# Query head norm moved from the queries to the exponential: a per-token scale instead of a per-column factor, in the attention stage of a decoder step

## The chip, the core and the metric

The kernel runs on one core of one Trainium2 chip. The core has a matrix engine (PE, TensorE), a vector engine (DVE), a scalar engine (ACT), GpSimd (POOL), a sync engine (SP) that issues nearly all DMAs here, 16 DMA engines, an on-chip memory with 128 partitions (SBUF) and matrix-product buffers (PSUM). Each engine runs its own instructions in its own order and waits on semaphores for the others. The metric is the device time of one execution in microseconds (us); lower is better.

## The reference, cut to what matters

One step of a two-layer decoder trunk over 512 prompt tokens and 32 sample tokens (8 requests of 4), model width 1024, 8 heads of 128. The first layer ends with a shared key, value and log-forget value; the second layer attends to them. The change is in the attention of the second layer:

```python
q = rmsnorm((xn @ att_w_q[j]).reshape(bsz, L, N_HEADS, HEAD_DIM), q_norm[j])
...
s = jnp.einsum('bqhd,bkhd->bhqk', qb, k).astype(jnp.float32) * scale      # scale = HEAD_DIM ** -0.5
s = s + cq[..., :, None] - csum[..., None, :]                             # csum: running sum of log-forget
s = jnp.where(causal[None, None], s, -jnp.inf)
p = jax.nn.softmax(s, axis=-1).astype(v.dtype)
return jnp.einsum('bhqk,bkhd->bqhd', p, v)
```

`rmsnorm` divides each query, per token and head, by the root of the mean square of its 128 values and multiplies by a gain per value. The sample tokens do the same against 256 cached keys and 4 own ones.

## The kernel before, in words

Everything is held transposed: 128 features on the partitions, the 544 tokens (512 + 32) along the free axis. Every large product is done in three matmuls: each operand is split into a rounded high part (fp32r) and the remainder, and high x high, high x low and low x high are summed in PSUM (lines L285, L289, L291 for a projection tile: 8 blocks of the inner dimension x 3 x 2 column halves of 272 = 48 matmuls). ACT makes the high part, DVE subtracts for the low part (L241 and L242 for weights, L329 and L330 for activations, L341 and L342 where a gain goes in).

Buffers come from pools: 45 of a large kind (`big`), 8 of a token-row kind (`tmp`), 3 two-bank PSUM tiles (`ps`) and 2 one-bank ones (`pb`).

The attention of the second layer is written as a list of short steps (the string `ORDER`), one letter and a head or group number each; the instructions are emitted in that order, and a list scheduler then sets the final order on each engine from its own costs. The steps:

- `q` h: the query tile of head h, 48 matmuls; DVE multiplies it by the layer norm's factor (L1108), ACT squares it (L786).
- `s` hs: the sum of squares over each head. The 128 partitions are summed by matmuls against a block of ones, four heads in four 32-column strips of the PE array (L794); then on `[128 x 544]` rows ACT makes a first reciprocal root (L385) and DVE one correction step (L388, L391, L392); the rows are written to DRAM (L805).
- `n` h: the row of head h is read back, spread to 128 partitions (L810), and DVE multiplies the query by gain and row (L1118).
- `p` h: the split of the normed query in high and low (L329, L330). `f` h: the loads of the head's keys and values (L1153, L1154).
- `a` h: the scores. For each block of 128 tokens five matmuls into a `ps` tile: the forget term (L1169: a constant `L` of one head by the terms `R` of all heads), query by key (L1170 to L1172) and the causal mask (L1174); then, block by block, DVE takes the negated maximum (L1184), ACT the exponential with it as bias and the sum as a by-product (L1185), DVE the reciprocal (L1186), and ACT (L1190) or POOL (L1188) scales the row.
- `t` h: ten transposes on PE (L1200), then the splits of the result. `v` h: the product with the values (L1219 to L1221). `z`, `S`, `T`, `P`, `U`, `O`: the sample tokens (scores on L1246). `h`, `o`: the output projection (L1330 to L1337). `K`, `V`: loads of cache pages (L1127, L1138).

Two `ps` tiles hold the scores of one head and one more its transposes; with three in all, the scores of the next head start when exponentials of the last have read theirs. The next sections name lines of this kernel as L and a number below; lines of the changed kernel stand in the order listings and are said to be so.

## Time and profile before

| what | value |
|---|---|
| median of 3 runs | 1928.19 us (1927.69 to 1928.40) |
| the profiled execution's own time | 1928.06 us |
| its span in the profile | 1926.3 us |
| PE busy | 1904.8 us, 99% |
| DVE busy | 1457.4 us, 76% |
| ACT busy | 949.2 us, 49% |
| POOL busy | 143.4 us, 7% |
| granted PE clock in each of 40 slices | 9 tenths or more |

The span runs from the first to the last instruction that the profile shows; 1.76 us of the execution's own time lie outside it. Of matmuls the profile shows a start and a modelled end: they are pipelined, so the distance between two starts tells what one costs, and its own duration is longer. An fp32 matmul, which is not rounded to fp32r, leaves two records.

The query tiles begin at about 1347 us of the span, the first scores stand at 1390 us, and the output projection ends at about 1520 us.

### The profile page before, as it was taken

The page shows a single profiled execution, that of the slowest core. Times are in us where ns is not written, and L with a number is a line of the kernel's source. Part 1 is how long each engine was busy: PE and PEld are TensorE (multiplying, and loading weights), DVE is VectorE, ACT ScalarE, POOL GpSimd, SP SyncE. Part 2 cuts the span into 40 slices and gives each one's busy share as a digit, 9 for nine tenths or more (in the row PEclk, how much of TensorE's full clock was granted, in tenths as well). Part 3 has the DMA queues.
Part 4 walks back from the last instruction along what each step waited for, and adds up shares of the span by engine and source line. Part 5 has one row for each costly group of instructions (what it writes and reads, how often), then busy time and mean ns, then how long its engine had stood idle before and what let it go on. Part 6 is the DMA issues. An engine that isn't in the chain of part 4 may idle for free.

```text
span 1926.3 us, 39008 instructions
## 1 busy us (share of the span) xinstructions
PE 1904.8 (99%) x16508; PEld 1869.8 (97%) x16508; DVE 1457.4 (76%) x1799; ACT 949.2 (49%) x1396; POOL 143.4 (7%) x190
## 2 busy tenths in 40 slices
PE   9999999999999999999999999999999999999999
PEld 8999999999999999999999999999977899999999
DVE  7987877556788887767578887876476888878774
ACT  7544434424554544454466454444374754444461
POOL 0000000410100000023000000002131300000020
PEclk9999999999999999999999999999999999999999
DMA  5233234312223233431484232324769332332431
GB/s 196 90 102 121 89 118 156 99 48 88 89 88 116 91 115 120 132 112 46 149 305 150 98 129 71 128 95 128 226 214 332 99 110 84 109 113 86 140 108 47
DMA packets 98048, 237.62 MB, mean 123 GB/s; under 512 B 12130, under 2 KB 29826, under 8 KB 97874
## 3 DMA queue, kind: packets, MB, share of 16 engines
q1 hardware_dynamic: 97730, 235.09, 36.9%
q8 instruction: 130, 2.13, 0.5%
q14 instruction: 44, 0.36, 0.1%
q10 hardware_dynamic: 144, 0.04, 0.0%
HBM read 218.65 MB, written 16.44 MB: 122 GB/s over the span
## 4 chain that ended last, share of the span: by engine, by line
PE 89%; DVE 5%; ACT 2%; DMA 2%; issue 1%; SPq 0%; POOL 0%; ACTq 0%; DVEq 0%
PE ps L538 31%; PE ps L285 15%; PE ps L291 15%; PE ps L289 15%; PE pb L538 5%; DVE big L242 1%; DMA tmp<-rows 1%; ACT big L241 1%; PE ps L891 1%; PE ps L892 1%; PE ps L893 1%; DVE big L227 1%; DVE big L330 0%; PE ps L1285 0%; PE ps L676 0%
## 5 line engine op out<-in xcount | busy, mean ns | idle before, releaser
L538 PE MATMUL ps<-big,big 128*128 128x272 f32 x5616 | 668.5, 279 | 3.1 <-ACT tmp L546 1.7
L538 PEld LDWEIGHTS ps<-big,big 128*128 128x128 f32 x5616 | 658.4, 189 | 3.9 <-ACT tmp L546 2.1
L242 DVE TENSOR_TENSOR big<-big,big 128x1024 fp32r<-128x1024 f32 (+2 forms) x505 | 582.1, 1156 | 86.7 <-ACT big L241 85.9
L241 ACT CAST big<-big 128x1024 fp32r<-128x1024 f32 (+2 forms) x505 | 482.4, 975 | 325.1 <-DVE big L227 251.5
L285 PE MATMUL ps<-big,big 128*128 128x272 f32 x2668 | 530.1, 280 | 3.0 <-ACT big L241 1.4
L291 PE MATMUL ps<-big,big 128*128 128x272 f32 x2668 | 528.4, 279 | 2.9 <-DVE big L242 2.8
L289 PE MATMUL ps<-big,big 128*128 128x272 f32 x2668 | 527.5, 279 | 0.6 <-DVE big L342 0.6
L285 PEld LDWEIGHTS ps<-big,big 128*128 128x128 f32 x2668 | 407.2, 189 | 7.9 <-ACT big L241 4.5
L291 PEld LDWEIGHTS ps<-big,big 128*128 128x128 f32 x2668 | 406.9, 189 | 5.0 <-DVE big L242 4.5
L289 PEld LDWEIGHTS ps<-big,big 128*128 128x128 f32 x2668 | 406.9, 189 | 1.0 <-DVE big L342 1.0
L370 POOL TENSOR_TENSOR st<-st,tmp 128x544 f32<-128x544 f32 (+1 forms) x63 | 87.4, 1388 | 1472.4 <-ACT tmp L368 1472.1
L227 DVE TENSOR_TENSOR big<-big,big 128x1024 f32<-128x1024 f32 x156 | 190.1, 1219 | 0.0
L577 DVE SCALAR_TENSOR_TENSOR big<-ps,big 128x544 f32<-128x544 f32 x128 | 92.5, 722 | 104.1 <-PE ps L291 103.2
L546 ACT COPY tmp<-ps 128x544 f32<-128x544 f32 x117 | 71.5, 611 | 111.3 <-PE ps L538 111.3
L496 DVE TENSOR_TENSOR big<-big,st 128x1088 f32<-128x1088 f32 x88 | 113.5, 1291 | 3.3 <-ACT big L560 2.0
L538 PE MATMUL pb<-big,big 128*128 128x272 f32 x936 | 114.8, 279 | 0.0
L538 PEld LDWEIGHTS pb<-big,big 128*128 128x128 f32 x936 | 111.3, 189 | 0.0
L499 ACT ACTIVATE big<-big 128x544 f32<-128x544 f32 x88 | 57.8, 659 | 88.0 <-DVE big L496 87.9
L341 ACT ACTIVATE big<-big,gains 128x544 fp32r<-128x544 f32 (+1 forms) x80 | 55.4, 702 | 91.3 <-DVE big L577 55.2
L330 DVE TENSOR_TENSOR big<-big,big 128x544 fp32r<-128x544 f32 (+1 forms) x112 | 79.3, 714 | 22.7 <-ACT big L329 22.5
L342 DVE SCALAR_TENSOR_TENSOR big<-big,gains,big 128x544 fp32r<-128x544 f32 (+1 forms) x80 | 64.6, 817 | 24.3 <-ACT big L341 24.3
L329 ACT CAST big<-big 128x544 fp32r<-128x544 f32 (+1 forms) x112 | 71.2, 643 | 12.2 <-DVE big L502 7.4
(218 smaller groups left out, 1388.5 us busy)
## 6 DMA issues: line engine op xcount, KB each, us to landing
big<-in_w SPq DMA_DIRECT2D x156, 512.0 KB
big<-in_w2b SPq DMA_DIRECT2D x96, 384.0 KB
big<-in_w13p SPq DMA_DIRECT2D x16, 512.0 KB
big<-in_w2a SPq DMA_DIRECT2D x16, 512.0 KB
big<-in_win SPq DMA_DIRECT2D x16, 512.0 KB
big<-in_wg SPq DMA_DIRECT2D x16, 512.0 KB
big<-in_ck SPq DMA_DIRECT2D x16, 512.0 KB
big<-in_cv SPq DMA_DIRECT2D x16, 512.0 KB
```

Of the source, the lines that this page charges most:

```text
L227: self.nc.vector.tensor_tensor(t, a, b, ALU.add if op == "+" else ALU.subtract)
L241: self.nc.scalar.copy(hi, src)
L242: self.nc.vector.tensor_tensor(lo, src, hi.bitcast(F32), ALU.subtract)
L285: i = nc.tensor.matmul(o, wh, xh[:, b], start=s, stop=False)
L289: nc.tensor.matmul(o, wh, xl[:, b], start=False, stop=False)
L291: nc.tensor.matmul(o, wl, xh[:, b], start=False, stop=e)
L330: self.nc.vector.tensor_tensor(pair[:, 1, cols], src, pair[:, 0, cols].bitcast(F32), ALU.subtract)
L370: nc.gpsimd.tensor_tensor(acc[:, cols], acc[:, cols], sq, ALU.add)
L496: tt(g, g, rstd.unsqueeze(1).broadcast_to([P, 2, T]), ALU.mult)
L538: nc.tensor.matmul(turns(dst[w]), a[:, c], woven(b), start=k in "152" and kp == 0 and n == 0, stop=kp == NKP - 1 and n == 2, skip_group_ch ...
L546: nc.scalar.copy(t["r" + k], t["C" if k == "5" else "A"])
L577: nc.vector.scalar_tensor_tensor(halves(h[c]), whole(out), 0.5, halves(h[c]), ALU.mult, ALU.add)
```

## The change

The norm of a query is one number per token and head. Before, it is multiplied into the query. Now the scores are made from the query without it, with the tokens on the partitions, and the number is given to the exponential as its scale (one per partition, so one per token). Since the forget term is added inside PSUM, before that scale, it is divided by it first: the matmul's stationary operand, which was a constant, now holds the reciprocal of the scale per token, in a high and a low part. The query token's own running sum, the same for all keys of a row, is left out for the prompt. In detail:

- Sums of squares (step `s`, now 0 and 1, four heads each): the squared query is now the stationary operand, 128 tokens at a time, and one column of ones is streamed. 16 matmuls per group give a `[128 tokens x 16]` table; the second group has two more for the sample tokens, whose squares POOL makes.
- The reciprocal root is then made on this table by DVE alone: a first guess from the bits and three correction steps (12 instructions), three more for the high and low part of the reciprocal, and two copies that spread these to 512 columns. No row goes through DRAM any more.
- A step `r` is new: 16 transposing matmuls in four 32-column strips bring the table into the form of the stationary operand `L`, and ACT copies it.
- Step `n` is gone. The split of step `p` multiplies by the gain.
- The forget terms are loaded per head (`R`), as `L` was before; the stage that makes them has one ACT and one DVE instruction less.
- The softmax works on pairs of token blocks: two maxima, one multiplication by the scale, two exponentials, one reciprocal for both, two scalings.
- Sample: the queries are multiplied by the gain where they were copied (POOL), and the addition of the bias multiplies by the scale.
- `ORDER`: the `s` of the first four heads follows q3, the last query tile comes after the first head's scores, the second `s` after the second head's scores, and the pages K1 are loaded later.

```diff
 ORDER = """
-q0 K3 K2 K0 q1 q2 q3 K1 s0123 n2 n3 n1 q4 f1 p1 q5 q6 f0 n0 q7 p2 p0 f3 f2 a0 s4567 p3 t0 a1 v0 a2
-t1 n4 n5 a3 n7 n6 t2 p4 z f4 K5 v1 v2 f5 p5 K6 t3 a4 S0 v3 f6 h00 p6 V5 f7 a5 K7 t4 K4 v4 t5 p7 V7
+q0 K3 K2 K0 q1 q2 q3 s0 f0 q4 r0 p0 f1 q5 p1 q6 a0 q7 p2 f2 t0 a1 s1 v0 p3 f3 a2 t1 K1 a3 r1 t2
+p4 z f4 K5 v1 v2 f5 p5 K6 t3 a4 S0 v3 f6 h00 p6 V5 f7 a5 K7 t4 K4 v4 t5 p7 V7
...
             def take(p=p, qc=box["q"][:, h % 2, :]):
                 box["last"] = nc.vector.tensor_tensor(halves(qc), whole(p), halves(box["rstd"]), ALU.mult)
                 q[h], sqs[h] = qc, self.square(qc)
+                for g in range(2):
+                    new = qc[:, SEQ + 16 * g:SEQ + 16 * g + 16].rearrange("p (b t) -> p b t", t=NQ)
+                    nc.gpsimd.tensor_tensor(ss[g].rearrange("p (b h t) -> p b h t", h=NH, t=NQ)[:, :, h, :], new, new,
+                                            ALU.mult)
...
-        def stat(*hs):
-            bcs.update(zip(hs, self.head_rows([sqs.pop(h) for h in hs], P ** -0.5)))
-
-        def norm(h):
-            bc = bcs.pop(h)()
-            with self.tc.issue_after(box["last"].ins):
-                nc.vector.scalar_tensor_tensor(q[h], q[h], self.gain(G_Q), bc, ALU.mult, ALU.mult)
+        def stat(g):
+            dve, n = nc.vector, 18 if g else 16
+            t = self.pb()
+            for j in range(4):
+                sq = sqs.pop(4 * g + j)
+                for i in range(4):
+                    nc.tensor.matmul(t[:, 4 * j + i:4 * j + i + 1], sq[:, i * P:i * P + P], self.ones[:, 0:1],
+                                     start=True, stop=True)
+            for k in range(2 * g):
+                nc.tensor.matmul(t[:, 16 + k:17 + k], ss[k], self.ones[:, 0:1], start=True, stop=True)
+            y, w = sc[:, 16 * g:16 * g + n], cols[:, 40 + 64 * g:104 + 64 * g]
+            x, u = w[:, :n], w[:, 18:18 + n]
+            dve.tensor_scalar(x, t[:, :n], P * EPS, None, ALU.add)
+            dve.tensor_scalar(u.bitcast(I32), x.bitcast(I32), 1, None, ALU.logical_shift_right)
+            dve.tensor_scalar(y.bitcast(I32), u.bitcast(I32), -1, 0x5f3759df, ALU.mult, ALU.add)
+            for _ in range(3):
+                dve.tensor_tensor(u, y, y, ALU.mult)
+                dve.scalar_tensor_tensor(u, u, -0.5, x, ALU.mult, ALU.mult)
+                dve.scalar_tensor_tensor(y, u, 1.5, y, ALU.add, ALU.mult)
+            hi = w[:, 36:52].bitcast(F32R)
+            x, u = x[:, :16], u[:, :16]
+            dve.tensor_tensor(x, x, y[:, :16], ALU.mult)
+            dve.tensor_copy(hi, x)
+            dve.tensor_tensor(u, x, hi.bitcast(F32), ALU.subtract)
+            box["w", g] = w = self.tmp()[:, :SEQ]
+            v = w.rearrange("p (n h q) -> p n h q", h=NH, q=NQ)
+            for k, part in enumerate((hi.bitcast(F32), u)):
+                dve.tensor_copy(v[:, :, :, 2 * k:2 * k + 2], part.unsqueeze(2).unsqueeze(3).broadcast_to([P, 16, NH, 2]))
+
+        def rows(g):
+            w, t = box.pop(("w", g)), self.pb()
+            for i in range(4):
+                for j in range(4):
+                    nc.tensor.matmul(t[32 * j:32 * j + 32, i * P:i * P + P], w[:, 128 * j + 32 * i:128 * j + 32 * i + 32],
+                                     self.ident, start=True, stop=True, skip_group_check=True)
+            nc.scalar.copy(self.L[:, g, :SEQ], t)
...
         def prep_q(h):
-            st["q", h] = self.big(F32R)
-            self.split_pair(st["q", h], q[h][:, :SEQ], slice(0, SEQ))
+            st["q", h] = self.prep(q[h], G_Q, cols=slice(0, SEQ))
...
-                nc.tensor.matmul(into, self.L[h % 4][:, qs], blocks_woven(self.R[:, 0, :w]), start=True, stop=False)
+                nc.tensor.matmul(into, self.L[:, h // 4, qs], blocks_woven(self.R[h % 4][:, :w]), start=True, stop=False)
...
-                m, l = self.sm(1), self.sm(1)
+                if i % 2 == 0:
+                    m2, l2, r2 = self.sm(2), self.sm(2), scale[:, 4 * h + i:4 * h + i + 2]
+                    for k in range(2):
+                        nc.vector.tensor_reduce(m2[:, k:k + 1], S[i // 2][:, k, :w + P * k], AX.X, ALU.max, negate=True)
+                    nc.vector.tensor_tensor(m2, m2, r2, ALU.mult)
+                k = slice(i % 2, i % 2 + 1)
                 p = self.tmp()
-                nc.vector.tensor_reduce(m, sc, AX.X, ALU.max, negate=True)
-                nc.scalar.activation(blocks_halves(p[:, :w]), blocks_unwoven(sc), AF.Exp, bias=m, accum_out=l)
-                nc.vector.reciprocal(l, l)
-                if i in (1, 2):
-                    nc.gpsimd.tensor_scalar(p[:, :w], p[:, :w], l, None, ALU.mult)
-                else:
-                    nc.scalar.activation(p[:, :w], p[:, :w], AF.Copy, scale=l)
+                nc.scalar.activation(blocks_halves(p[:, :w]), blocks_unwoven(sc), AF.Exp, bias=m2[:, k], scale=r2[:, k],
+                                     accum_out=l2[:, k])
                 ps.append(p)
+                if i % 2:
+                    nc.vector.reciprocal(l2, l2)
...
```

How this stands on the engines, word for word as the built programs have it (line, operation, what it writes and reads with buffer numbers, size, count). First PE before, from the end of the fourth query tile (`ps_16502`) to the start of the fifth (`ps_16615`):

```order
L291 MATMUL ps_16502<-big_16218,big_16371 128x272 x2
L794 MATMUL pb_16577<-tmp_16385,ones 32x272
L794 MATMUL pb_16577<-tmp_16437,ones 32x272
L794 MATMUL pb_16577<-tmp_16494,ones 32x272
L794 MATMUL pb_16578<-tmp_16385,ones 32x272
L794 MATMUL pb_16578<-tmp_16437,ones 32x272
L794 MATMUL pb_16578<-tmp_16494,ones 32x272
```

The same place now; the fifth tile is `ps_16601`, and L1122 is the matmul of the new `stat`, L1150 that of `rows`:

```order
L291 MATMUL ps_16502<-big_16212,big_16371 128x272 x2
L1122 MATMUL pb_16556<-ones,tmp_16379 128x1 x4
L1122 MATMUL pb_16556<-ones,tmp_16433 128x1 x4
L1122 MATMUL pb_16556<-ones,tmp_16492 128x1 x4
...
L289 MATMUL ps_16601<-big_15955,big_16437 128x272 x2
L1122 MATMUL pb_16556<-ones,tmp_16552 128x1 x4
L291 MATMUL ps_16601<-big_15955,big_16438 128x272 x2
...
L291 MATMUL ps_16601<-big_16212,big_16438 128x272 x2
L1150 MATMUL pb_16656<-consts,tmp_16588 32x128 x16
```

Twelve one-column matmuls stand ahead of the fifth tile and four inside it, and the transposes of the table behind it.

Second, DVE before, from the fourth query's evacuation (L1108) on:

```order
L1108 TENSOR_TENSOR big_16492<-ps_16502,st_16296 128x544
L388 SCALAR_TENSOR_TENSOR tmp_16588<-st_16587 128x544
L391 SCALAR_TENSOR_TENSOR tmp_16588<-pb_16577,tmp_16588 128x272
L391 SCALAR_TENSOR_TENSOR tmp_16588<-pb_16578,tmp_16588 128x272
L392 SCALAR_TENSOR_TENSOR st_16587<-tmp_16588,st_16587 128x544
L1108 TENSOR_TENSOR big_16664<-ps_16615,st_16296 128x544
L1108 TENSOR_TENSOR big_16664<-ps_16681,st_16296 128x544
L1118 SCALAR_TENSOR_TENSOR big_16492<-big_16492,gains,tmp_16600 128x544
L1118 SCALAR_TENSOR_TENSOR big_16492<-big_16492,gains,tmp_16603 128x544
L1118 SCALAR_TENSOR_TENSOR big_16306<-big_16306,gains,tmp_16606 128x544
L330 TENSOR_TENSOR big_16672<-big_16306,big_16672 128x512
L242 TENSOR_TENSOR big_16676<-big_16500,big_16675 128x1024
```

And now (L1103 is the evacuation; the three lines L1132 to L1134 come three times):

```order
L1103 TENSOR_TENSOR big_16490<-ps_16502,st_16290 128x544
L1128 TENSOR_SCALAR cols<-pb_16556 128x16
L1129 TENSOR_SCALAR cols<-cols 128x16
L1130 TENSOR_SCALAR cols<-cols 128x16
L1132 TENSOR_TENSOR cols<-cols 128x16
...
L1140 TENSOR_TENSOR cols<-cols 128x16
L1144 COPY tmp_16588<-cols 128x128x2 x2
L1103 TENSOR_TENSOR big_16650<-ps_16601,st_16290 128x544
L342 SCALAR_TENSOR_TENSOR big_16674<-big_16300,gains,big_16674 128x512
L242 TENSOR_TENSOR big_16682<-big_16500,big_16681 128x1024
```

Seventeen small instructions stand where four wide ones stood, and the three multiplications that read the rows (`tmp_16600` to `tmp_16606`) are gone from between the evacuations and the weight split L242.

Third, PE now, from the first head's last scores (`ps_16806`) past the eighth query tile (`ps_16858`) to the first head's transposes (`ps_16919`, L1241), the second head's scores (`ps_16943`, `ps_16944`) and the first head's values (L1260). Before, the last query tile stood ahead of nearly all of the first head's scores, and the values of the first head between the scores of the third:

```order
L1207 MATMUL ps_16806<-neg,identr 128x256
L285 MATMUL ps_16858<-big_15937,big_16681 128x272 x2
...
L291 MATMUL ps_16858<-big_16212,big_16682 128x272 x2
L1241 MATMUL ps_16919<-consts,tmp_16833 128x128
L1241 MATMUL ps_16919<-consts,tmp_16835 128x128 x2
L1202 MATMUL ps_16943<-big_16221,big_16219 128x256
...
L1122 MATMUL pb_16990<-ones,tmp_16652 128x1 x4
L1202 MATMUL ps_16944<-big_16221,big_16219 128x384
...
L1125 MATMUL pb_16990<-ones,big_16220 128x1 x2
L1260 MATMUL pb_17027<-big_16931,big_16592 128x512
```

The whole query tile lies between the first head's scores and its transposes, and the one-column matmuls of the second group lie between the second head's scores and the first head's values.

## The prediction

> **What bounds the kernel now.** I read the page's head first, then the chain that ended last, then the attention by windows.

> ```profile
> span 1926.3 us, 39008 instructions
> PE 1904.8 (99%) x16508; PEld 1869.8 (97%) x16508; DVE 1457.4 (76%) x1799; ACT 949.2 (49%) x1396; POOL 143.4 (7%) x190
> PE 89%; DVE 5%; ACT 2%; DMA 2%; issue 1%; SPq 0%; POOL 0%; ACTq 0%; DVEq 0%
> ```

> The matrix engine is idle for 21.5 of 1926.3 us and carries 89% of the chain. A change of the norm can therefore give two things: fewer or more microseconds of PE work, and fewer or more PE waits. Whatever it saves on DVE, ACT or in DMA counts only as far as it ends such a wait. The windows say where waits are left (columns: stretch, its length, busy time of PE, PEld, DVE, ACT and POOL, granted clock, DMA share, GB/s):

> ```profile
> 1369.50:1391.30 21.80, 21.38 (x177) 18.74 (x175) 8.69 (x13) 5.83 (x9) 1.43 (x6) 1.00 0.46 166
> 1391.30:1428.20 36.90, 33.30 (x227) 29.08 (x227) 26.57 (x65) 26.41 (x69) 11.04 (x20) 1.00 0.50 156
> 1428.20:1477.00 48.80, 47.89 (x550) 43.08 (x548) 32.30 (x76) 29.57 (x76) 14.22 (x30) 1.00 1.06 354
> 1477.00:1500.00 23.00, 21.23 (x187) 13.48 (x186) 17.88 (x33) 12.31 (x37) 9.25 (x19) 1.00 0.72 243
> 1500.00:1566.00 66.00, 61.59 (x513) 59.96 (x513) 56.63 (x74) 43.71 (x66) 7.91 (x12) 1.00 0.28 89
> ```

> From the fourth query tile's end (1369.5) to the first sample scores (1428.2), where five heads' scores and three heads' values are done, PE idles 0.42 + 3.60 = 4.0 us; up to 1477 another 0.9. After that come 1.8 and 4.4 us, which belong to the sample values, the output projection and the next feed-forward block. The change edits none of those, and by the order listings PE's program is the same there but for one transpose. So the question is settled between 1369.5 and 1477. Who ends the waits up to 1428.2:

> ```profile
> PE ps L1169 <- ACT tmp L1185: 2.1, 3, 1.3
> PE ps L1200 <- ACT tmp L1190: 0.7, 1, 0.7
> PE ps L291 <- DVE big L242: 0.4, 1, 0.4
> ```

> The largest is not the norm but the scores of the next head (L1169), which wait until an exponential has read a `ps` tile. The norm's own path is in the chain of waits (start, length, what):

> ```profile
> 1373.72 0.59 PE pb L794 x2
> 1374.33 0.96 ACT st L385 x2
> 1375.31 0.74 DVE tmp L388
> ...
> 1378.36 1.14 DMA rows<-st
> 1379.58 0.55 SPq L810
> 1380.23 6.62 DMA tmp<-rows
> 1386.87 1.49 DVE big L1118 x2
> ...
> 1389.98 1.24 DVE big L242
> 1391.26 0.50 PE ps L291 x2
> ```

> It takes 14.7 us from the last sum of squares (1373.7) to the multiplied queries (1388.4), 6.6 of it one spread read. But PE fills that time with query tiles, and all that reaches PE is a weight split (L242) that DVE made late.

> **The change part by part.** First PE work, which no other engine can hide. *Taken away*: 16 matmuls L794, in four batches. The first batch, and its neighbours, on the timeline:

> ```profile
> 1369.41 0.40 PE L291 MATMUL ps<-big,big 128*128 128x272 f32 x2
> 1369.74 1.12 PE L794 MATMUL pb<-tmp,ones 128*32 128x272 f32 x12
> 1370.79 0.50 PE L285 MATMUL ps<-big,big 128*128 128x272 f32 x2
> 1371.12 0.39 PE L289 MATMUL ps<-big,big 128*128 128x272 f32 x2
> ```

> From 1369.41 to 1371.12 are 1.71 us. Two pairs of such matmuls need 0.46 (four at the pitch of 0.116 that the row of L538 below gives), so the batch costs 1.25 with the two changes of column tiling, 1.05 of it between its own start and the next L285. Four batches: 5.0 us less. *Added*: 34 matmuls with a 128 x 128 fp32 stationary operand and one streamed column. The program before has four of the same form, in the shared key and value stage:

> ```profile
> L864 PE MATMUL pb<-consts,st x8: 242/250/250, 915.4 to 916.2; 128*128 128x1 f32 x8
> ```

> Eight records (two per fp32 matmul) start in 0.78 us, so one record costs 0.11 us although it streams one column: the weight load sets it. 68 records: 7.6 us more (between 2.0 by the 0.03 us of a strip record in the next row and 7.9 by a full 272-column one; I take the row of the same form). [...] *Added* too: 32 transposing matmuls of `rows` in four strips. Nearest row, in the chain: the sample scores, in the same four strips and with the same 128 streamed columns.

> ```profile
> 1456.87 3.68 PE pb L1246 x128
> ```

> 128 records take 3.68 us, so 64 take 1.84, plus 0.2 (the 1.25 less 1.05 above) for each of three groups, since the second table's matmuls stand in two: 2.5 us. The score matmuls keep their number and sizes (a constant `L` by common terms becomes a common `L` by terms per head). PE work: -5.0 + 7.6 + 2.5 = **+5.1 us**.

> Second the waits. The stretch from 1369.5 to 1428.2 must be compared as a whole, since drained matmuls count as busy. What its work costs by pitch:

> ```profile
> 1057.99 2.78 PE pb L538 x24
> 1425.24 0.28 PE L1171 MATMUL ps<-big,big 128*128 128x256 f32 x1
> 1425.35 0.28 PE L1172 MATMUL ps<-big,big 128*128 128x256 f32 x1
> 1426.73 0.38 PE L1169 MATMUL ps<-big,big 128*128 128x512 f32 x1
> 1426.95 0.38 PE L1170 MATMUL ps<-big,big 128*128 128x512 f32 x1
> ```

> Pitches are 0.116 for 272 columns, 0.11 for 256, 0.22 for 512, and in between, 0.16, for 384. A query tile is 48 x 0.116 = 5.6 us; a head's scores 12 x 0.11 + 4 x 0.16 + 4 x 0.22 = 2.85; its values 3 x (0.22 + 0.16 + 2 x 0.11) = 1.8; its ten transposes, at 0.11, 1.1. Four tiles, five score sets, four sets of transposes, three of values and the batches: 22.4 + 14.2 + 4.4 + 5.4 + 5.0 = 51.4 of 58.7 us. So 7.3 us of the stretch are waits and what restarts cost behind them. That is all there is to gain here, and 5.1 is spent.

> How much goes? I walked through the changed orders with the durations above. The first table's chain is 15 small dependent DVE instructions and two copies. Nearest rows, from the forget stage:

> ```profile
> 933.84 1.37 DVE L988 SCALAR_TENSOR_TENSOR tmp<-tmp 128x40 f32<-128x40 f32 x6
> 935.71 0.24 DVE L993 COPY tmp<-tmp 128x160 f32<-128x160 f32 x1
> ```

> Six in 1.37 is 0.23 each: 3.4 us, and two copies of 256 elements at some 0.35: 4.1 us, no DMA. The fifth tile has 38 matmuls left behind its sums (4.4 us), so `rows` finds its table with 0.3 us to spare. If that cover failed, PE would stand for the lateness itself, a few tenths. The first scores then start at 1369.5 + 3.6 (16 one-column matmuls) + 1.1 (`rows`) + 16.7 (three tiles) = 1391, about where they stand now, but without the wait for L242. The eighth tile gives 5.6 us of PE work while the first head's softmax runs (ACT is busy 26.4 us for over four heads and all else in its window, so 6 us a head at most), and its transposes hardly wait; then the second sums (3.8 us) cover the second head's softmax. These were the largest waits. From the third head on no filler is left. The second table's DVE chain (4.1 us) stands in DVE's queue ahead of the third head's maxima, and the paired softmax holds a `ps` tile longer. ACT and DVE are each busy 26.5 of 36.9 us, so neither is full; with three `ps` tiles it is the latency that counts. Going down the two queues I find 1.5 us of waits for the fourth head's scores and 1.1 for the fifth's, and allow 1.0 for restarts. So 3.6 stay and 3.7 of 7.3 us go. Sum: **+5.1 - 3.7 = +1.4 us** up to 1428. From there to 1477 the 0.9 us may shrink or grow by a few tenths; I take nothing.

> At nothing I put: the eight L1118 and the wide row steps gone from DVE, and ACT's two L385 per group (they lie beside PE work; without cover they would be worth the waits counted above and no more); the gain in the split, a multiply-and-subtract for a subtraction of the same width (DVE has 10 us to spare in the second window); POOL's 16 squares and 16 scaled copies of 16 columns for 16 copies (L1233, all in POOL's idle time, 12.5 busy of 58.7); one ACT and one DVE instruction less in the forget stage, where PE does not wait. On SP the row writes and reads go. One queue place matters: the keys of the fifth head are issued behind the forget terms of the eighth, which overwrite those that the fourth head's scores read.

> ```profile
> 1418.88 0.52 SPq L1153 DMA_DIRECT2D big<-kd  x1
> ```

> So it stood before too, but there the fifth head's scores ran at 1425, 6 us later; now they would come some 4 us behind the fourth's. 512 KB at the 350 GB/s of the full windows is 1.5 us plus the start, so it should land just in time: 0 to 1.5 us.

> **The sum.** 1928.06 (the profiled execution; 1926.3 span and 1.76 outside) + 1.4 = 1929.5. The median is 0.13 above that execution, which I ignore: **1929.5 us**.

> **The rivals.** *Slower*: the paired softmax, at the scores from the third head on. Every head's first exponential now waits for a second maximum and a product, and carries a second operand per partition.

> ```profile
> L1184 DVE TENSOR_REDUCE sm<-ps 128x1 f32<-128x256 f32 x4 | 1.6, 405 | 0.0
> L1190 ACT ACTIVATE tmp<-tmp,sm 128x512 f32<-128x512 f32 x4 | 2.9, 713 | 0.3 <-DVE sm L1186 0.3
> L1224 ACT CAST big<-pb 128x512 fp32r<-128x512 f32 x3 | 1.6, 580 | 0.2 <-PE pb L1221 0.2
> ```

> The maximum is 0.41 us, the product 0.2 like the small DVE rows. No row shows an exponential with a scale per partition; a copy with one takes 0.71 against 0.58 without, so 0 to 0.13 us each, and I took 0 above. [...] Together 0.6 + 0.1 us per head, for six heads 4.2 us, from the point where PE has no more work per head (2.85 + 1.8 + 1.1 = 5.75 us) than a head's way through DVE and ACT takes: 1929.5 + 4.2 = 1933.7. For it: L1169 waiting for L1185 is the largest wait of before. Against it: ACT and DVE have less else to do.

> *Faster*: the fillers end all waits, up to 1477 as well. Then 1928.06 + 5.1 - 7.3 - 0.9 = 1925, and a little less DVE work could take another microsecond from the feed-forward start: 1924. For it: DVE, which has 4 wide multiplications less in this stretch, and no DMA on the path. Against it: from the third head on nothing new stands between scores and transposes.

> *No gain at all*: the waits only move behind other instructions and the work comes on top: 1928.06 + 5.1 = 1933.2. For it: an engine order made by a scheduler that has filled such gaps before. Against it: the fillers stand exactly at the two largest waits.

> **How the numbers follow.** A measurement of this kernel can tell about 0.2%, 3.9 us, from no change; so 1924.3 and 1932.0 are the bounds of same. Forecast (1926.5 to 1932.0): 0.67. Slower rival 0.11 and no gain 0.10, both beyond 1932.0: slower 0.21. Faster 0.12. The range goes from all waits of the stretch gone (1928.06 + 5.1 - 7.3 = 1925.9), less 0.7 of the 0.9 behind it, to none gone (1933.2) and a few tenths: 1925.2 to 1933.4. The one-column matmuls at their lower bound (5.6 us less work) lie outside it: the row of the same form speaks against them.

> **What would show it.** Right: L794 gone, the one-column matmuls about 0.11 us apart; no `rows` DMA in the chain between 1374 and 1391; first scores near 1391; PE busy up by some 5 us over the span, its idle time down by 3 to 4; idle left where scores wait for exponentials from the fourth head on. Wrong: one-column matmuls at 0.03 us (the work falls), or idle PE in front of `rows` (the DVE chain is late), or waits for keys at the fifth head, or PE idle behind 1477 changed by over 1 us, which I hold fixed.

## The result, and the profile after

The changed kernel takes 1934.02 us (median of 8, 1929.74 to 1935.68) against 1927.68 for the kernel before (median of 8, 1926.90 to 1928.40): 1.0029 times as long, 95% interval 1.0020 to 1.0038. The forecast was 1929.5 us, "same", in a range up to 1933.4. So the kernel became slower, by 0.3%, and the median lies 0.6 us outside the range.

One thing must be known to read the number. The eight executions of the same program differ in the matrix engine's mean granted clock, and the time goes with it: three at 1.000 took 1929.74 to 1929.94 us, two at 0.997 took 1933.94 and 1934.10, three at 0.996 took 1935.30 to 1935.68. At full clock the forecast is met within 0.4 us. What it did not see is the clock.

The profiled execution took 1935.51 us, 1933.7 of it span. The page's head and the windows of the changed kernel (columns as in the prediction):

```profile
span 1933.7 us, 39203 instructions
PE 1914.9 (99%) x16608; PEld 1884.1 (97%) x16608; DVE 1455.2 (75%) x1816; ACT 949.8 (49%) x1393; POOL 148.7 (8%) x206
```

```profile
1369.50:1391.30 21.80, 21.80 (x184) 21.47 (x184) 8.87 (x24) 6.49 (x9) 2.98 (x12) 0.84 0.22 77
1391.30:1431.60 40.30, 39.31 (x300) 37.38 (x299) 24.01 (x72) 24.17 (x61) 11.82 (x21) 0.92 0.44 134
...
1507.00:1573.00 66.00, 61.59 (x513) 59.97 (x513) 56.62 (x74) 43.82 (x66) 7.90 (x12) 1.00 0.28 89
```

PE is busy 10.1 us longer than before and idle 2.7 us less (18.8 against 21.5). In the last row, the 66 us that lead into the next feed-forward block, nothing changed: 61.59 us busy in both kernels. The news is the column behind POOL: the clock is 0.84 and 0.92 in the first two stretches, where it was 1.00. Cut finer, at the moments when the clock changes:

```profile
1368.67:1372.08 3.41, 3.41 (x32) 3.41 (x32) 0.72 (x1) 0.66 (x1) 0.99 (x4) 1.00 0.72 275
1372.08:1378.90 6.82, 6.82 (x33) 6.82 (x32) 2.77 (x17) 0.00 (x0) 0.00 (x0) 0.50 0.00 1
1378.90:1382.31 3.41, 3.41 (x49) 3.28 (x50) 0.75 (x3) 0.00 (x0) 0.00 (x0) 1.00 0.00 0
1406.21:1409.62 3.41, 3.41 (x30) 3.30 (x28) 2.15 (x6) 1.71 (x8) 0.93 (x1) 1.00 0.39 106
1409.62:1416.44 6.82, 6.82 (x29) 6.55 (x30) 4.14 (x19) 2.78 (x7) 1.50 (x2) 0.50 0.30 114
1416.45:1419.86 3.41, 3.41 (x38) 3.14 (x41) 2.70 (x8) 1.60 (x6) 0.00 (x0) 1.00 0.10 24
```

Twice the clock falls to one half in these stretches, for 6.8 us each time. All four changes lie on one grid of 3.413 us: between them are 6.827, 30.72 and 6.827 us in the trace's clock records, which is two, nine and two steps, and no longer step fits all three; the next change, 1.9 us before the span's end, lies 151 steps further on. One step of it is called a window of the grid below. What PE did in these windows, from the timeline (start, length, what):

```profile
1369.18 2.73 PE L1122 MATMUL pb<-ones,tmp 128*128 128x1 f32 x24
1371.77 0.52 PE L285 MATMUL ps<-big,big 128*128 128x272 f32 x2
...
1373.90 1.70 PE L1122 MATMUL pb<-ones,tmp 128*128 128x1 f32 x8
...
1407.20 2.91 PE L1122 MATMUL pb<-ones,tmp 128*128 128x1 f32 x24
1409.98 0.99 PE L1125 MATMUL pb<-ones,big 128*128 128x1 f32 x4
```

Both spells begin at the end of a window that is for the most part filled with one-column matmuls: 1369.18 to 1371.77 is 2.59 of the first window's 3.41 us, 1407.20 to 1409.62 is 2.42 of the second's. By its busy column PE is at work all the time. The two spells, 13.65 us in all at half clock, are 6.8 us of lost work; the changed kernel's spans in this execution and at full clock differ by 5.8 (1933.7 and 1927.9), so about 1 us came back in waits that the slower stretch filled (PE is idle for 18.8 us here, and for 19.8 in e6_wide8 below, which has the same order on PE and no spell).

### The profile page after: what moved, and what is told of

It is laid out like the page before. It is cut to its first block, busy times and chain, and to the rows that moved or that the text cites. A ratio compares the mean times of both kernels' runs of the same rounds, so it can differ in the third digit from the quotient of the medians.

```text
span 1933.7 us, 39203 instructions
## 1 busy us (share of the span) xinstructions
PE 1914.9 (99%) x16608; PEld 1884.1 (97%) x16608; DVE 1455.2 (75%) x1816; ACT 949.8 (49%) x1393; POOL 148.7 (8%) x206
## 4 chain that ended last, share of the span: by engine, by line
PE 91%; DVE 4%; ACT 2%; issue 1%; DMA 1%; SPq 0%; POOL 0%; ACTq 0%; DVEq 0%; POOLq 0%
PE ps L538 31%; PE ps L285 15%; PE ps L291 15%; PE ps L289 15%; PE pb L538 5%; DVE big L242 1%; PE ps L891 1%; PE ps L892 1%; PE ps L893 1%; ACT big L241 1%; DVE big L227 1%; DVE big L330 0%; PE ps L1328 0%; PE pb L1122 0%; PE ps L676 0%
## 5 line engine op out<-in xcount | busy, mean ns | idle before, releaser
L538 PE MATMUL ps<-big,big 128*128 128x272 f32 x5616 | 668.5, 279 | 3.1 <-ACT tmp L546 1.7
L538 PEld LDWEIGHTS ps<-big,big 128*128 128x128 f32 x5616 | 658.4, 189 | 3.9 <-ACT tmp L546 2.1
L242 DVE TENSOR_TENSOR big<-big,big 128x1024 fp32r<-128x1024 f32 (+2 forms) x505 | 581.8, 1155 | 86.5 <-ACT big L241 85.6
L285 PE MATMUL ps<-big,big 128*128 128x272 f32 x2668 | 531.4, 280 | 2.9 <-ACT big L241 1.3
L291 PE MATMUL ps<-big,big 128*128 128x272 f32 x2668 | 529.0, 280 | 2.2 <-DVE big L242 1.9
L289 PE MATMUL ps<-big,big 128*128 128x272 f32 x2668 | 528.5, 280 | 0.3 <-DVE big L342 0.3
L285 PEld LDWEIGHTS ps<-big,big 128*128 128x128 f32 x2668 | 408.3, 189 | 7.1 <-ACT big L241 4.0
L291 PEld LDWEIGHTS ps<-big,big 128*128 128x128 f32 x2668 | 407.9, 189 | 3.6 <-DVE big L242 3.6
L289 PEld LDWEIGHTS ps<-big,big 128*128 128x128 f32 x2668 | 407.8, 189 | 0.7 <-DVE big L342 0.7
L538 PE MATMUL pb<-big,big 128*128 128x272 f32 x936 | 114.8, 279 | 0.0
L538 PEld LDWEIGHTS pb<-big,big 128*128 128x128 f32 x936 | 111.3, 189 | 0.0
L341 ACT ACTIVATE big<-big,gains 128x544 fp32r<-128x544 f32 (+2 forms) x88 | 61.3, 704 | 90.9 <-DVE big L577 55.1
L342 DVE SCALAR_TENSOR_TENSOR big<-big,gains,big 128x544 fp32r<-128x544 f32 (+2 forms) x88 | 70.5, 809 | 26.3 <-ACT big L341 26.1
L330 DVE TENSOR_TENSOR big<-big,big 128x544 fp32r<-128x544 f32 (+1 forms) x104 | 73.7, 715 | 20.5 <-ACT big L329 20.4
L329 ACT CAST big<-big 128x544 fp32r<-128x544 f32 (+1 forms) x104 | 66.3, 645 | 8.6 <-DVE big L502 7.4
```

Of the source, the lines that this page charges most:

```text
L242: self.nc.vector.tensor_tensor(lo, src, hi.bitcast(F32), ALU.subtract)
L285: i = nc.tensor.matmul(o, wh, xh[:, b], start=s, stop=False)
L289: nc.tensor.matmul(o, wh, xl[:, b], start=False, stop=False)
L291: nc.tensor.matmul(o, wl, xh[:, b], start=False, stop=e)
L330: self.nc.vector.tensor_tensor(pair[:, 1, cols], src, pair[:, 0, cols].bitcast(F32), ALU.subtract)
L538: nc.tensor.matmul(turns(dst[w]), a[:, c], woven(b), start=k in "152" and kp == 0 and n == 0, stop=kp == NKP - 1 and n == 2, skip_group_ch ...
```

## The experiments

My theory after the result, **idle array**: a matmul that loads 128 x 128 weights and streams one column keeps the engine busy and the array idle; when a window holds more than some two thirds of that, the clock is halved. The rivals: it is the run of weight loads or the number of such matmuls; it is another part of the change (the strip transposes, the paired softmax, the shorter waits); or it comes with the phase alone, whatever PE does. All times below are medians; the kernel before, run beside them, was at 1927.6, 1927.38 and 1927.42 us in the three sets.

**The same loads with more columns.** `e1_wide`: 64 columns of ones are streamed, each matmul's other 63 results are overwritten by the next.

```diff
-  nc.tensor.matmul(t[:, 4 * j + i:4 * j + i + 1], sq[:, i * P:i * P + P], self.ones[:, 0:1],
+  nc.tensor.matmul(t[:, 4 * j + i:4 * j + i + 64], sq[:, i * P:i * P + P], self.onesr[:, 0:64].bitcast(F32),
```

> The changed kernel, but each of the 34 sum matmuls streams 64 columns of ones instead of one (63 of the 64 results are overwritten by the next matmul); loads, count and order stay. Theory 'idle array': the matrix engine's clock is halved because in these groups the array itself computes for one column per weight load, so that it counts as idle; with 64 columns it counts as busy, the granted clock stays 1.000 and every run takes about 1930 us (1929.8 plus 68 times what a record costs more than 0.112 us; at most +2). Rival 'weight loads': back-to-back full weight loads as such, or the group's place in the program, bring the clock down; then the runs fall on the changed kernel's two levels again, about 1930 at clock 1.000 and 1934 to 1936 at 0.996 to 0.997.

1928.60 us (11 runs, 1928.09 to 1930.38; ratio to before 1.0006, 0.9997 to 1.0015), clock 1.000 in the profile and nothing below 0.998 in any run. The groups stand where they stood (24 records from 1369.53, eight from 1373.37) and take as long:

```profile
1369.53 2.79 PE L1122 MATMUL pb<-onesr,tmp 128*128 128x64 f32 x24
...
1373.37 1.00 PE L1122 MATMUL pb<-onesr,tmp 128*128 128x64 f32 x8
```

The windows of the grid that hold the first group (its 24 records fill 2.59 us of the first, 1369.18 to 1372.59) stay at full clock:

```profile
1369.18:1376.01 6.83, 6.83 (x63) 6.83 (x62) 2.09 (x9) 0.66 (x1) 0.99 (x4) 1.00 0.34 129
```

That is as much of one window as in the changed kernel, where the clock fell. So it is neither the loads nor the place nor the phase of the grid. Three of the eleven runs, at a clock of 0.998 or 0.999, lie 0.8 to 1.8 us above the median. One window at half clock costs at most 1.7 us and 0.0009 of the mean clock (an estimate: 3.41 us at 0.50, in a span of 1926.8), so a single such window in these runs is not excluded; none of them was profiled. `e6_wide8` is the same edit with 8 columns.

> As e1_wide, but 8 columns streamed instead of 64. Theory 'idle array' with a bound somewhere between 1 and 64 columns: if 8 columns in 0.112 us (a tenth of the columns that the same time streams in a tile matmul's 272 at 0.116) still count as idle, two levels as in the changed kernel, median 1932 to 1936; if 8 count as busy, about 1928.6 and clock 1.000. I expect idle. Rival 'phase alone' (e1_wide was lucky): both e1_wide and this one on two levels with no difference.

1933.93 us (5 runs): 1929.62 at clock 1.000, the other four 1933.23 to 1935.62 at 0.996 to 0.998, close to the changed kernel's levels. Judged by these levels, eight columns per load still count as idle, and 64 do not; "phase alone" falls, since one of the two kernels has the levels and the other has not. The profile happened to be taken of the run at full clock. All its 16608 PE records stand in the changed kernel's order, so it shows that kernel without spells (page's head, waits from 1365 to 1510: total, times, longest):

```profile
span 1927.8 us, 39203 instructions
PE 1908.0 (99%) x16608; PEld 1877.4 (97%) x16608; DVE 1455.0 (75%) x1816; ACT 949.7 (49%) x1393; POOL 148.6 (8%) x206
```

```profile
PE ps L1202 <- ACT tmp L1222: 1.4, 3, 0.7
PE ps L1380 <- POOL big L1360: 1.3, 1, 1.3
PE ps L1202 <- DVE big L330: 0.7, 1, 0.7
...
```

And of its timeline the first sums, the first scores and the second sums, with the group of the strip transposes (busy, mean ns, idle before):

```profile
1368.96 2.74 PE L1122 MATMUL pb<-onesr,tmp 128*128 128x8 f32 x24
...
1390.42 0.27 PE L1202 MATMUL ps<-big,big 128*128 128x256 f32 x1
...
1403.67 2.74 PE L1122 MATMUL pb<-onesr,tmp 128*128 128x8 f32 x24
```

```profile
L1150 PE MATMUL pb<-consts,tmp 128*32 128x128 f32 x64 | 2.6, 276 | 0.0
```

The grid's edges, continued from the clock records at the start of this trace, fall at 1367.72, 1371.13, 1401.86 and 1405.27. They cut both groups, so that no window holds more than 2.2 us of them: this run escapes by its phase.

**The same matmuls, apart.** `e3_spread`: 28 of the 34 sum matmuls go two at a time behind every six matmuls of the next query tile, and the first table's rows a tile later.

```diff
-q0 K3 K2 K0 q1 q2 q3 s0 f0 q4 r0 p0 f1 q5 p1 q6 a0 q7 p2 f2 t0 a1 s1 v0 p3 f3 a2 t1 K1 a3 r1 t2
+q0 K3 K2 K0 q1 q2 q3 m0 f0 q4 s0 p0 f1 q5 r0 p1 q6 a0 m1 q7 p2 f2 t0 a1 s1 v0 p3 f3 a2 t1 K1 a3 r1 t2
...
                 nc.tensor.matmul(o, wl, xh[:, b], start=False, stop=e)
+            for _ in range(2):
+                if self.between:
+                    self.between.pop(0)()
```

> The changed kernel with the same 34 sum matmuls, but 28 of them two at a time behind every six matmuls of the next query tile (heads 0 to 3 in the fifth tile, heads 4 to 6 in the eighth); six stay in a group. The first table comes a tile later and its rows one tile later. Theory 'idle array': no 3.4 us have more than some 1.4 us of one-column work, so the clock stays 1.000 and all runs take about 1930 us (1928.5 to 1931.5). Rival 'weight loads' or 'number of such matmuls': two levels as for the changed kernel, median 1933 to 1935. Rival 'the table is late': clock 1.000 but 2 to 6 us longer because the first scores wait for the rows.

1929.46 us in 11 runs, all between 1929.13 and 1929.63, clock 0.999 to 1.000 in each (ratio to before 1.0009, 1.0000 to 1.0018). Same number of one-column records, one level of time, 4.6 us below the changed kernel's median:

```profile
1370.85 0.50 PE L1121 MATMUL pb<-ones,tmp 128*128 128x1 f32 x4
1371.21 0.48 PE L287 MATMUL ps<-big,big 128*128 128x272 f32 x2
...
1371.99 0.50 PE L1121 MATMUL pb<-ones,tmp 128*128 128x1 f32 x4
```

Here 0.36 of every 1.14 us are one-column records, an estimate of 1.1 us in a window. It is the share of a window that counts, not the number.

**The suspected cost by itself.** `e4_dummy`: the kernel before with two groups of 16 one-column matmuls on its own squares; one small DVE copy reads each result, which is not used further.

```diff
-  bcs.update(zip(hs, self.head_rows([sqs.pop(h) for h in hs], P ** -0.5)))
+  ts = [sqs.pop(h) for h in hs]
+  bcs.update(zip(hs, self.head_rows(ts, P ** -0.5)))
+  t = self.pb()
+  for j in range(4):
+      for i in range(4):
+          nc.tensor.matmul(t[:, 4 * j + i:4 * j + i + 1], ts[j][:, i * P:i * P + P], self.ones[:, 0:1],
+                           start=True, stop=True)
+  nc.vector.tensor_copy(self.sm(1), t[:, :1])
```

> The kernel before, unchanged but for 32 more one-column matmuls in two groups of 16, on the same squares and at the place of its own sums, whose results go unused. Theory 'idle array': 7.2 us of work, and in most runs one or two half-clock spells of 6.8 us (2 to 3.4 us of loss each): 1934.9 us at clock 1.000 in some runs, 1937 to 1941 at 0.996 to 0.998 in the others. Rival 'another part of the change': clock 1.000 and 1934.9 us in every run.

1939.07 us (5 runs, 1936.02 to 1941.21; ratio 1.0056, 1.0042 to 1.0070), the clock between 0.995 and 0.998. Nothing of the change is in this kernel but those matmuls (and the copies), and the spells are there (windows of the grid, each group's window and what follows):

```profile
1379.68:1383.09 3.41, 3.41 (x32) 3.41 (x32) 0.16 (x1) 0.00 (x0) 0.00 (x0) 1.00 0.82 197
1383.09:1386.50 3.41, 3.41 (x17) 3.41 (x16) 0.69 (x1) 0.00 (x0) 0.00 (x0) 0.50 0.78 249
1410.40:1413.81 3.41, 3.41 (x34) 3.41 (x33) 0.00 (x0) 0.00 (x0) 0.00 (x0) 1.00 0.07 22
1413.81:1420.63 6.82, 6.33 (x24) 5.24 (x24) 4.44 (x16) 5.03 (x16) 2.15 (x2) 0.50 0.01 2
```

Of the five windows at half clock in this trace these are three. One more stands behind waits (last section), and one at 7.52 to 10.93 us, near the start of the span, where nothing was edited. I had expected some runs at clock 1.000; there were none in five. A group of 16 is an estimated 3.6 us without a break (32 records at the 0.11 us of L864's row), longer than a window, so a cut by the grid leaves at least 1.8 us on one side; whether 1.8 would be enough no run shows.

**What the sums cost.** `e2_few`: one sum matmul per group in place of 16 or 18; the norms of the other tokens and heads are left out, all behind them stays.

```diff
-  for j in range(4):
-      sq = sqs.pop(4 * g + j)
-      for i in range(4):
-          nc.tensor.matmul(t[:, 4 * j + i:4 * j + i + 1], sq[:, i * P:i * P + P], self.ones[:, 0:1],
-                           start=True, stop=True)
-  for k in range(2 * g):
-      nc.tensor.matmul(t[:, 16 + k:17 + k], ss[k], self.ones[:, 0:1], start=True, stop=True)
+  sq = [sqs.pop(4 * g + j) for j in range(4)][3]
+  nc.tensor.matmul(t[:, :n], sq[:, :P], self.ones[:, :n], start=True, stop=True)
```

> The changed kernel with one sum matmul per group of four heads in place of 16 or 18 (the norms of the other tokens and heads are left out, the table, its rows and the softmax stay as they are). Theory 'idle array': 32 matmuls of two records at 0.112 us are gone, 7.2 us, and with them the half-clock spells: about 1922.6 us, clock 1.000 in all runs. Rival 'the spells come from another part' (the strip transposes of the table, the paired softmax, the shorter waits): 7.2 us less but spells as before, most runs at 1927 to 1928.5 and a clock of 0.996 to 0.997. Rival 'hidden work': the sums lie in waits of the matrix engine; then less than 4 us are gained.

1925.77 us (11 runs, 1925.35 to 1927.53), clock 0.999 or 1.000: none of the changed kernel's spells of two windows, so these do not come from another part. (Two runs at 0.999 took 1927.46 and 1927.53, as one window at half clock would make them; they were not profiled.) But from the changed kernel's 1929.8 at full clock this is 4.0 us, not the 7.2 that the records measure. Most of the other 3.2 went into waits: from 1391 to 1431 PE is busy 36.44 us against 37.80 in e1_wide, and from 1431 to 1480 46.42 against 48.27. The largest from 1391 to 1445 (e2_few, then e1_wide):

```profile
PE ps L1197 <- ACT tmp L1217: 1.7, 2, 1.1
PE ps L1197 <- DVE sm L1214: 1.3, 1, 1.3
PE ps L1197 <- DVE big L330: 0.7, 1, 0.7
...
```

```profile
PE ps L1241 <- POOL tmp L1230: 1.2, 1, 1.2
PE pb L1260 <- DVE big L330: 0.6, 1, 0.6
PE ps L1202 <- ACT tmp L1222: 0.4, 1, 0.4
...
```

These rows are 3.7 us against 2.2: score matmuls (L1197 is L1202 of the changed kernel) come earlier and wait for exponentials, maxima and splits. So the second group of sums, which lies between scores and values, was partly free.

**The query tile behind the first head.** `e10_q7_first` is e1_wide with the eighth tile put back ahead of the first head's scores.

```diff
-... q6 a0 q7 p2 f2 t0 a1 s1 v0 ...
+... q6 q7 a0 p2 f2 t0 a1 s1 v0 ...
```

> e1_wide with the eighth query tile put back ahead of the first head's scores, as in the kernel before. The tile is 5.6 us of matrix work that lies between the first head's scores and its transposes. Theory 'filler': without it the transposes wait for the first head's exponentials; the first head's chain of two maxima, multiplication, exponential and division is 3 to 4 us long, so the kernel takes 2 to 4 us longer, 1930.5 to 1932.5. Rival 'any order does' (the next waits shrink by as much): 1928 to 1929.5.

1932.16 us (9 runs, 1931.66 to 1933.45), 3.6 us longer than e1_wide: the tile is a filler, as expected. The first head's transposes (L1241) now wait for its exponentials, and the wait itself has a second price:

```profile
1401.44 0.33 PE L1241 MATMUL ps<-consts,tmp 128*128 128x128 f32 x1 [2.27 <-ACT tmp L1232]
```

```profile
1399.23:1402.64 3.41, 1.20 (x10) 1.16 (x11) 1.35 (x4) 3.16 (x10) 0.92 (x1) 1.00 0.07 19
1402.64:1406.05 3.41, 3.41 (x14) 3.23 (x13) 0.95 (x4) 1.97 (x7) 1.24 (x1) 0.50 0.01 2
```

PE is idle 2.21 us of a window, and the next window runs at half clock. Here no one-column matmul is near; an idle engine does the same.

`e11_q7_later` moves the tile the other way, behind the second head's scores, and `e12_q67` moves the seventh tile too, one tile behind each of the first two heads. Both start from the e9_f32r_pair that is described below (1925.92 us).

```diff
-... q5 p1 q6 a0 q7 p2 f2 t0 a1 s1 v0 p3 f3 a2 ...
+... q5 p1 q6 a0 p2 f2 t0 a1 q7 s1 v0 p3 f3 a2 ...     (e11_q7_later)
+... q5 a0 p1 q6 t0 a1 p2 f2 q7 s1 v0 p3 f3 a2 ...     (e12_q67)
```

> e9_f32r_pair with the eighth query tile one place further on, behind the second head's scores instead of the first's; the second group's sums and all behind it follow. Theory 'filler where it waits': the remaining waits (fourth and fifth head, about 3 us in e1_wide) come later by a head's work and shrink by 1 to 2 us; but the first head's transposes lose their cover (2 to 3 us). I expect 0 to +3 us against e9_f32r_pair. Rival: the vector and scalar engines get ahead and 1 to 2 us go.

> e9_f32r_pair with the first head's scores ahead of the seventh query tile too, which then lies behind them, and the eighth behind the second head's scores: one tile of 5.6 us behind each of the first two heads. Theory 'filler': each of the first two heads' softmax has a tile to hide in, the heads behind them start with the vector and scalar engines further ahead: 0.5 to 2.5 us less than e9_f32r_pair, if the table's rows are there in time (the first scores come 5.6 us earlier, 0.3 us was to spare by the forecast's count and a tile of 5.6 us now lies between). Rival 'table late': the first scores wait for the rows, 1 to 5 us more.

1931.34 us (11 runs, 1929.70 to 1932.34) and 1927.68 (11 runs, 1927.50 to 1928.03): 5.4 us longer, where I had allowed 0 to 3, and 1.8 us longer, where I had expected 0.5 to 2.5 less. In the profile of e11_q7_later, its slowest run, PE waits 2.5 us for the first head's exponentials and 2.5 at the fourth head's scores, and a half-clock window stands behind each (2.18 us idle from 1392.45 to 1395.86 and 2.19 from 1412.93 to 1416.34; the clock of the next window is 0.50 both times). In e12_q67 the wait of 2.5 us at the fourth head's scores is there too, but the grid's cut falls inside it and the clock stays:

```profile
1408.41:1411.82 3.41, 1.69 (x13) 1.39 (x12) 2.85 (x14) 1.42 (x4) 0.00 (x0) 1.00 0.70 200
1411.82:1415.23 3.41, 2.68 (x19) 2.63 (x20) 3.34 (x14) 1.67 (x7) 0.48 (x1) 1.00 0.53 127
```

The changed kernel's place for the tile was the best of the four tried. Nor did the first scores of e12_q67 stand for the table: its loss is at the fourth head.

**The paired softmax.** `e5_single` is e1_wide with maximum, exponential, reciprocal and division block by block, as in the kernel before.

```diff
-  if i % 2 == 0:
-      m2, l2, r2 = self.sm(2), self.sm(2), scale[:, 4 * h + i:4 * h + i + 2]
-      for k in range(2):
-          nc.vector.tensor_reduce(m2[:, k:k + 1], S[i // 2][:, k, :w + P * k], AX.X, ALU.max, negate=True)
-      nc.vector.tensor_tensor(m2, m2, r2, ALU.mult)
...
+  m, l, r = self.sm(1), self.sm(1), scale[:, 4 * h + i:4 * h + i + 1]
+  nc.vector.tensor_reduce(m, sc, AX.X, ALU.max, negate=True)
+  nc.vector.tensor_tensor(m, m, r, ALU.mult)
+  nc.scalar.activation(blocks_halves(p[:, :w]), blocks_unwoven(sc), AF.Exp, bias=m, scale=r, accum_out=l)
+  nc.vector.reciprocal(l, l)
```

> The changed kernel with 64 streamed columns in its sum matmuls (as in e1_wide, 1928.6 us) and with the softmax of the kernel before: maximum, exponential and reciprocal block by block, where the change takes two blocks together. Theory 'pairing holds up the exponential': with 64 columns the matrix engine still waits some 3 us for exponentials and score tiles between 1413 and 1425; block by block the first exponential of a head starts one maximum (0.5 us) earlier, and 1 to 3 us go: 1925.6 to 1927.6. Rival 'pairing costs nothing' (the waits are those of the score tiles, as before the change): 1928 to 1929.5, the 32 more small DVE instructions (0.16 us each) lying beside other work.

1933.87 us (6 runs, 1932.88 to 1935.37): 5.3 us longer than e1_wide, where I had expected 1 to 3 less. Two more pairs say the same. `e7_spread_single` is the edit on e3_spread:

> The spread sums of e3_spread (1929.46 us, clock 1.000) together with the block-by-block softmax of the kernel before. Theory 'pairing holds up the exponential': 1926.5 to 1928.5. Rival 'pairing costs nothing': 1929 to 1930.

1932.51 (11 runs, 1930.89 to 1933.02), 3.1 us longer. `e8_f32r` is the edit on e9_f32r_pair:

> As e5_single, but the squares are stored rounded to the one-pass type (fp32r), so that a sum matmul is one record and not two (the sample tokens' two stay as they are). Sums lose precision by that. Theory 'work': 32 records of 0.112 us less than e5_single, 3.6 us, if nothing else takes their place: e5_single minus 3.6. Theory 'the sums partly fill waits' (e2_few gave back 4 of 7.2 us): e5_single minus 1.8 to 2.2. A one-pass matmul of 64 columns could also take longer than 0.112 us, which the trace shows.

1930.48 (11 runs, 1929.22 to 1931.57), 4.6 us longer than its partner; and 3.4 us shorter than e5_single, which bears out the 3.6 of the 32 records that it lacks. My theory on the pairing fell, with its sign. DVE's timeline at one late head shows what stands behind it (e5_single first, then e1_wide):

```profile
1418.22 0.28 DVE L1217 TENSOR_REDUCE sm<-ps 128x1 f32<-128x128 f32 x1
1418.54 0.16 DVE L1218 TENSOR_TENSOR sm<-sm,cols 128x1 f32<-128x1 f32 x1
1419.30 0.16 DVE L1220 RECIPROCAL sm<-sm 128x1 f32<-128x1 f32 x1 [0.60 <-ACT tmp L1219]
1419.74 0.16 DVE L1220 RECIPROCAL sm<-sm 128x1 f32<-128x1 f32 x1 [0.28 <-ACT tmp L1219]
1419.82 0.40 DVE L1217 TENSOR_REDUCE sm<-ps 128x1 f32<-128x256 f32 x1
```

```profile
1414.90 0.62 DVE L1218 TENSOR_REDUCE sm<-ps 128x1 f32<-128x128 f32 x2
1415.55 0.16 DVE L1219 TENSOR_TENSOR sm<-sm,cols 128x2 f32<-128x2 f32 x1
1415.95 0.17 DVE L1226 RECIPROCAL sm<-sm 128x2 f32<-128x2 f32 x1 [0.24 <-ACT tmp L1222]
```

Block by block, the reciprocals stand in DVE's queue ahead of the next block's maximum and wait for exponentials, so the second maximum (1419.82) comes 1.6 us behind the first. In pairs both maxima are done before anything waits. How much of the 3 to 5 us this queue makes was not measured by itself. Part of the loss is again the clock: several short waits add up to a window that is less than half busy, and the next runs at 0.50:

```profile
1422.76:1426.17 3.41, 1.55 (x7) 0.74 (x6) 2.89 (x8) 2.93 (x9) 1.48 (x4) 1.00 0.82 255
1426.17:1429.58 3.41, 3.41 (x13) 3.14 (x14) 0.65 (x1) 0.55 (x1) 0.00 (x0) 0.50 1.12 348
```

**A version of its own.** `e9_f32r_pair`: e1_wide with the squares rounded to fp32r when they are stored, so that a sum matmul is one record: the first 12 matmuls of a group leave 12 records in its trace, 24 in e1_wide's. The sums are then made of rounded squares, which the change's are not.

```diff
-  q[h], sqs[h] = qc, self.square(qc)
+  q[h], sqs[h] = qc, self.tmp(F32R)
+  nc.scalar.activation(sqs[h], qc, AF.Square)
...
-  nc.tensor.matmul(t[:, 4 * j + i:4 * j + i + 64], sq[:, i * P:i * P + P], self.onesr[:, 0:64].bitcast(F32),
+  nc.tensor.matmul(t[:, 8 * j + 2 * i:8 * j + 2 * i + 64], sq[:, i * P:i * P + P], self.onesr[:, 0:64],
```

> e1_wide (64 streamed columns, the change's paired softmax; 1928.6 us) with the squares rounded to the one-pass type, so 32 records fewer. Theory 'work': 32 times 0.112 = 3.6 us less, 1925.0. Theory 'the sums partly fill waits' (e2_few gave 4.0 of 7.2 us): 1.8 to 2.2 less, 1926.4 to 1926.8. Both: below the 1927.5 of the kernel before, clock 1.000. Paired against block by block: 4 us below the 1929.2 to 1931.6 of e8_f32r if pairing really gains (e1_wide against e5_single), about equal if that difference came from something else.

1925.92 us (11 runs, 1925.43 to 1928.06), 2.7 below e1_wide: between "work" and "the sums partly fill waits". Against the kernel before, 1927.42, the ratio is 0.9993, 0.9984 to 1.0002: the lowest median of a complete kernel here, but the interval reaches above 1, so a gain is not shown. Against the changed kernel's 1934.02 it is 8.1 us.

## Why the prediction was right and wrong

**The work, +5.1, and the waits, -3.7.** Right in sum at full clock: the changed kernel's runs at 1.000 lie at 1929.74 to 1929.94, and e6_wide8, which shows it at that clock, has a span of 1927.8, 1.5 above the 1926.3 of before; +1.4 was forecast. The single prices hold: 24 one-column records from 1369.18 to 1371.77 are 0.108 us each (0.11 forecast). The four groups of sums take 7.3 us in e6_wide8, from each one's start to the next matmul's (7.6 forecast). The strip transposes took 2.6 us (2.5). But two signs that the prediction named did not come: PE busy was to rise by some 5 us over the span and its idle time to fall by 3 to 4, and in e6_wide8 they are +3.2 and -1.7. As I read it, the forecast reckoned by pitches, which put a drained pipeline's restart to the waits, while the busy row counts matmuls to their modelled ends; the sum does not depend on that, the split does. No run tests this reading, so the split of +5.1 and -3.7 stays unproven beyond the prices above; if the reading is wrong, two errors of about 2 us cancelled and the sum was luck.

**Where the waits stay.** Right. The scores start at 1390.42 in e6_wide8 (1391 forecast); no wait stands before the fourth head's scores (PE is busy for all 39.50 us from 1369.5 to 1409), so the table's rows came in time; what remains from there on is waits for exponentials and splits (L1202, 2.1 us over the fourth to sixth head; 2.6 forecast for the fourth and fifth). The filler step held as well: without the tile (e10_q7_first) it costs 3.6 us. What was held fixed behind 1477 stayed: 61.59 us of PE in the last 66.

**What failed** is the step that prices the 34 sum matmuls by the row of L864 alone, "the weight load sets it" (that the columns do not is borne out: with 1, 8 and 64 of them, 24 records take 2.59, 2.60 and 2.59 us from the first start to the next matmul's), and goes on with the clock of 1.00 that the windows of before show. The row was of the same form, but only eight records long, 0.78 us; it could show the price and not what 2.6 us of them in one window do. In its place e1_wide, e3_spread and e4_dummy show: such a group halves the clock for one or two windows behind it, if enough of it falls into one window (2.4 us and more did so here). In the profiled execution that made 5.8 us of span (1933.7 against 1927.9), and over eight executions 4.1 to 4.3 us between the median and the runs at full clock. In the two traces of this order on PE the program meets the grid in another phase (the edge ahead of the first sums lies at 1368.67 in one, at 1367.72 in the other); from that, as I read it, come the levels of time and the three of eight runs that escape. The level at 0.997 was not profiled. The mechanism that was forecast happened; the term that was missing was not on the list, and none of the rivals had it.

**The rivals.** *Slower* had a time near the median (1933.7) by coincidence, for the wrong reason. Pairing the softmax does not cost 0.7 us a head, it gains: 5.3, 3.1 and 4.6 us in three pairs of kernels that differ in it alone. The prediction counted the longer way to the first exponential and overlooked what, block by block, stands in DVE's queue ahead of the second maximum. About the 0.1 us that it put down for the scale operand is there: the exponential of 512 columns takes 778 ns in the changed kernel's trace and 692 in that of before, the one of 128 columns 460 and 367. *No gain at all* (1933.2) falls by e6_wide8's idle time, which is 1.7 us lower than before, and by e10_q7_first, where the filler's 3.6 us are missing. *Faster* was out of reach while the sums cost what they do; e2_few shows that even without 32 of them only 4.0 of 7.2 us would come, since scores would then wait.

**What stays open.** e1_wide is 1.2 us below the changed kernel at full clock (1928.6 against 1929.8). On PE the strip transposes stand a little elsewhere in it and the waits differ (1.2 us for L1230 in place of 1.4 for L1222), but which of these makes the difference was not tried. Where the bound lies between 8 and 64 columns was not tried either. That the array's work is what is counted is the reading that fits all these runs; what they show is that the columns streamed per load decide.

## What to carry to other kernels

Look at what a group of matmuls streams, not only at what it takes: here 2.4 to 3.4 us of full weight loads in a window of 3.41, with one column behind each, acted like idleness, and what followed ran at a clock of 0.50, though the engine's busy row shows no gap (3.41 of 3.41 us). Stream more columns at the same price (here 24 records took 2.59 us with 64 as with one), or put two such matmuls at a time between wide ones (e3_spread: an estimated 1.1 us in a window, clock 0.999 to 1.000). When one program's runs lie on separate levels, read the granted clock of each first; and before a wait of 2 us is called worth 2 us, ask whether it will also cost the clock of the next window, as 2.21 us of idle time did in e10_q7_first.

## What the runs showed of the hardware that I had not expected

| kernel, window | in the window | clock after it |
|---|---|---|
| changed, 1368.67 | 2.59 us of one-column records | 0.50 |
| changed, 1406.21 | 2.42 us of one-column records | 0.50 |
| e4_dummy, 1410.40 | an estimated 3.4 us of one-column records (34 records on PE) | 0.50 |
| e1_wide, 1369.18 | 2.59 us of 64-column records | 1.00 |
| e6_wide8, 1367.72 | 2.2 us of 8-column records | 1.00 |
| e10_q7_first, 1399.23 | idle 2.21 us in one wait | 0.50 |
| e5_single, 1422.76 | idle 1.86 us in several waits | 0.50 |
| e12_q67, 1408.41 | idle 1.72 us | 1.00 |
| e4_dummy, 1430.88 | idle 1.66 us in several waits | 0.50 |
| before, 1401.94 | idle 1.40 us | 1.00 |

The rows that were not yet shown, of e6_wide8, e4_dummy and before:

```profile
1371.13:1374.54 3.41, 3.41 (x32) 3.41 (x32) 0.65 (x4) 0.00 (x0) 0.00 (x0) 1.00 0.03 12
```

```profile
1430.88:1434.29 3.41, 1.75 (x12) 1.07 (x10) 2.88 (x7) 3.32 (x9) 1.45 (x4) 1.00 1.00 200
1434.29:1437.70 3.41, 3.26 (x10) 2.62 (x11) 1.97 (x4) 0.38 (x1) 1.46 (x6) 0.50 1.09 365
```

```profile
1401.94:1405.35 3.41, 2.01 (x14) 1.53 (x13) 1.91 (x7) 1.67 (x8) 1.48 (x2) 1.00 0.08 22
```

By idle time alone the bound lies near half a window in these rows, and not sharply (1.72 us of 3.41 passed, 1.66 did not). 2.21 us in one gap and 1.86 in several sufficed, and so did a window without any gap. A spell lasted one window where a wide stream followed (e10_q7_first and e5_single: the window behind it is at 1.00); in the changed kernel each lasted two, and in both the first window at half clock held more one-column work (1.6 and 1.2 us). The second spell of e4_dummy lasted two windows as well, with 0.49 us idle in it. And the kernel before, with 1.40 us idle in one window, was itself by this table only a few tenths from a spell.
